# A float32 down product by seven block products in place of eight, on one Trainium2 core

## The chip, the core and the metric

The kernel runs on one core of one Trainium2 chip. It is one launch, with all inputs and outputs in HBM. The metric is the device time of the whole launch in microseconds (us); the profile adds the span, which is the time from the first to the last instruction on the core. Engines are named as in the profile: PE (TensorE), DVE (VectorE), ACT (ScalarE), POOL (GpSimd), SP (SyncE, here only a DMA queue). SBUF is the memory of the core's tiles, PSUM the accumulator memory that PE writes.

## What is computed

The reference is one step of a hybrid decoder layer over 576 tokens (512 of a prompt, 64 of requests), all in float32. Its first two thirds (input product, state space and attention branches, output product) are not touched by the change. What matters is the gated feed-forward layer at the end:

```python
h = rms_norm(x, g_ffn)
x = x + (jax.nn.silu(h @ w_gate_l) * (h @ w_up_l)) @ w_down_l
```

With `D` = 2048 model channels and `DFF` = 5632 hidden channels, the last product takes a hidden matrix g of 5632 x 576 (44 tiles of 128 channels, kept transposed) to 2048 x 576 (16 tiles of 128 channels).

## The kernel before, in words

**Precision.** A float32 product is made from three passes. Each operand is split into a rounded part and the rest: `split(hi, lo, src)` is an ACT copy (line 93) and a DVE subtraction `lo = src - hi` (line 96). For each pair of tiles PE then runs `hi*hi`, `hi*lo` and `lo*hi`. A matmul here has 128 x 128 weights and 288 tokens (`HALF`), so that one tile of 128 input channels by 128 output channels over all 576 tokens costs six matmuls.

**The gated layer** (lines 1775 to 1861) already uses Strassen's scheme in Winograd's form: tokens, input and output channels are each cut in two, and seven block products replace eight. The combined weights are made on DVE, and the results are combined on DVE out of PSUM. POOL does one multiplication `u<-u` of 128x576 for each tile of g and sends the tile to DRAM (`g_d`).

**The down product** (lines 1866 to 1912) is plain. The 44 tiles of g are taken in ranges: first 4 tiles, then five ranges of 8. In each range a loop runs over the 16 output tiles m; one job (m, range) is 4 or 8 input tiles by six matmuls into a pair of PSUM banks `pg`, and its evacuation `down_evac` is one DVE addition of 128x576 into the running sum `x1T` in SBUF, which starts as the layer's input. Weights come as `raw` tiles of four input tiles (128x512, 256 KB) from `w_down`; `advance` loads up to four and splits up to two ahead of the job that uses them. The next range's tiles of g are loaded (`g_in`, tile `u`) and split (`ghl`) between the jobs of the running range. After the last range, each finished row m is turned by five PE transposes, copied out of PSUM and stored; `pump` puts that work between the matmuls of later jobs. POOL has no work in the down product.

The order of instructions is set by a scheduling layer, which takes the program and orders each engine's instructions by priorities and buffers; each engine then runs its own list strictly in that order, and waits where a wait stands. So what follows an instruction in an engine's list also waits for it.

```python
def split(hi, lo, src):
    act(hi, src)
    tt(lo, src, hi, OP.subtract)
...
ranges = [(0, 4)] + [(k, k + 8) for k in range(4, nf, 8)]
...
x = x1T[:, m]
tt(v2(x), ps, v2(x), OP.add)
```

Of the kernel before, what the change touches and what calls it, by code (L numbers as in the profile page):

```python
# [37 lines left out]
class Pump:  # L38
    """Interleaves the emission of side work with the main stream of products."""
# [37 lines left out]
def hybrid_step_kernel(ctx, tc, x_prompt, x_sample, cache_k, cache_v, cache_win_k, cache_win_v,  # L77
# [164 lines left out]
    # rows of the paged caches to gather  # L242
# [52 lines left out]
    def rsqrt_small(x, scale):  # L295
        """(x * scale + eps) ** -0.5 in place for a few columns."""
        n = x.shape[1]
        ts(x, x, scale, OP.mult, EPS, OP.add)
        tt(x, x, mhalf[:x.shape[0], :n], OP.pow, G)

    def spread(out, r5):
        """Columns of tokens [128, 5] as rows on all partitions."""
        for s in range(2):
            ps = pt()
            for i, j in enumerate(((0, 1, 2, 3), (4,))[s]):
                n = 128 if j < 4 else TS
                tp(ps[:, i * 128:i * 128 + n], r5[:n, j:j + 1].to_broadcast([n, 128]), ident[:n, :n])
            (act if s == 0 else V.tensor_copy)(out[:, :TP] if s == 0 else out[:, TP:T], ps[:, :TP if s == 0 else TS])
# [54 lines left out]
    # =========================================================== products with the weights  # L363
# [40 lines left out]
    def run_group(group, ratio, before=None):  # L404
        """Emits the products of the group's jobs, side work of `ratio` times their time between them."""
        pss = [pt()[:, None, :] if j.small else pg() for j in group]
        n_k = sum(c[0] for c in group[0].chunks)
        k0 = 0
        for ci in range(len(group[0].chunks)):
            if before:  # L410
                before(ci)
            for job, ps in zip(group, pss):
                m = job.m
                nk, _, rhs = job.chunks[ci]
                i = state["i"]
# [12 lines left out]
        for job, ps in zip(group, pss):  # L428
            job.evac(ps[:job.m, :, :HALF])
# [26 lines left out]
    # =========================================================== keys, values, queries  # L456
# [166 lines left out]
    # =========================================================== constants used by the mixers  # L623
# [25 lines left out]
    def k_cmp_norm(pc, n):  # L649
        """RMS-normed rows (without the gain) of the compressed keys pc [n, 256]."""  # L650
# [88 lines left out]
    def tail(src, u, n, pa, hb, w2):  # L739
        """The second layer of a unit of blocks, and what becomes of its rows."""  # L740
# [39 lines left out]
    # =========================================================== attention of the new tokens  # L780
# [5 lines left out]
    def masked_bias(out, pattern, base, lim, cmp):  # L786
        """-slope * distance, far below any score where the distance fails the test."""
# [8 lines left out]
    def softmax_rows(s_, n, mx, gate, sums):  # L796
        """exp(s - max) * gate / sum in place over the first n columns of s_."""
# [9 lines left out]
    def sample_attn():  # L807
# [69 lines left out]
        # gates by row (g, r, i)  # L877
# [8 lines left out]
        # compressed branch of all requests, and the block that each row leaves out  # L886
# [33 lines left out]
        for b in range(8):  # L920
# [62 lines left out]
            def weigh(tiles, last=False):  # L983
                """tiles: (rows of P, its key count, the values)."""
# [71 lines left out]
    def to_ext(E, ps, w, rst):  # L1056
        """Columns of a product, scaled, into prompt and request rows with room for w - 1 earlier ones."""
# [59 lines left out]
    def ssd():  # L1117
# [70 lines left out]
        for c in range(5):  # L1188
# [3 lines left out]
            # token-major x * dt, its decayed copy, and B  # L1192
# [127 lines left out]
    # =========================================================== short convolution  # L1320
# [28 lines left out]
    # =========================================================== attention within the prompt  # L1349
    pp = None  # L1350

    def prompt_attn():
# [13 lines left out]
        def split_q(p, qb):  # L1366
            """For each half of the channels: the upper parts of its queries in its own partitions, the lower in the others."""
# [11 lines left out]
        for p in range(2):  # L1379
# [14 lines left out]
            for qb in range(4):  # L1394
# [4 lines left out]
                # compressed branch, eight heads at once  # L1399
# [182 lines left out]
    def slot(h, j, dt=F32):  # L1582
        """Channel tiles j and j + 8 of one half of the tokens, and then an operand's two parts in their place."""
# [55 lines left out]
    # ---- the gated layer's two products by Winograd's seven products of 2 x 2 blocks: the tokens, the output and  # L1639
    # the input channels are each cut in two; the operands of the tokens' side stay, those of the weights' side pass  # L1640
# [4 lines left out]
    def early(g):  # L1645
        """The first two products of group g, those that need the first half of the tokens only."""
# [219 lines left out]
    # ---- back to the model's channels  # L1866
# [3 lines left out]
    ranges = [(0, 4)] + [(k, k + 8) for k in range(4, nf, 8)]  # L1870
    gs = {}

    def g_in(f_):
        t_ = evt(T)
        nc.sync.dma_start(t_, g_d[f_])
        hl = fp.tile([128, 2, T], F32R, name="ghl", tag="ghl", bufs=16)
# [3 lines left out]
    def down_evac(m, last):  # L1880
        def f(ps):
            x = x1T[:, m]
            tt(v2(x), ps, v2(x), OP.add)
            if not last:
                return
            ot = evt(512).rearrange("p (a b) -> p a b", a=4)
            ots = fp.tile([TS, 128], F32, name="ots", tag="ots", bufs=2)

            def fin():
                yield  # L1890
                ps = pt()
                for j in range(4):
                    tp(ps[:, j * 128:(j + 1) * 128], x[:, j * 128:(j + 1) * 128], ident)
                act(ot, ps.rearrange("p (a b) -> p a b", a=4))
                ps = pt()
                tp(ps[:TS, :128], x[:, TP:T], ident)
                V.tensor_copy(ots, ps[:TS, :128])
                nc.sync.dma_start(dram(y_prompt, m * 128, [[D, 128], [128 * D, 4], [1, 128]]), ot)
                nc.sync.dma_start(dram(y_sample, m * 128, [[D, TS], [1, 128]]), ots)
                yield  # L1900
            pump.add(fin())
        return f

    jobs6 = [[Job(w_chunks(cols_src(w_down, D, m * 128, row0=k0 * 128), lambda k, k0=k0: gs[k0 + k], k1 - k0), 128,
                  down_evac(m, k1 == nf)) for m in range(KT)] for k0, k1 in ranges]
    for j in jobs6:
        add_jobs(j)
    for f_ in range(*ranges[0]):
        g_in(f_)
    for m in range(0, KT, 4):  # L1910
        nc.sync.dma_start(x1T[:, m:m + 4], x1_d[m:m + 4].rearrange("k p t -> p k t"))
    for n, j in enumerate(jobs6):
        nxt = list(range(*ranges[n + 1])) if n + 1 < len(ranges) else []
        for m, job in enumerate(j):
            if nxt and m >= 1 and m % (2 if n else 1) == 0:
                g_in(nxt.pop(0))
            run_group([job], 0.3)
        for f_ in nxt:
            g_in(f_)
    pump.drain()  # L1920
    close_pool(fg)
    close_pool(x1g)
    close_pool(fwg)
# [30 lines left out]
```

## Time and profile before

| | |
|---|---|
| median of 3 runs | 2958.08 us (2955.71 to 2959.1) |
| span of the profiled execution | 2957.9 us |
| PE busy | 2894.8 us, 98% of the span |
| DVE busy | 1867.6 us, 63% |
| ACT busy | 1158.4 us, 39% |
| POOL busy | 579.3 us, 20% |
| down product, first matmul to end of span | 2371.2 to 2957.9 us |

The profiled execution is one more execution than the three runs; its span, 2957.9 us, lies inside their range, and no other time is known of it. A busy share says how long an engine had an instruction in work over the whole span; since the program has stages with different limits, the stretch of the down product is read by itself.

### The profile page before, as it was taken

The numbers are of one execution on the slowest core, as the hardware profiler recorded it, in microseconds if no ns is written. First come the engines' busy times: TensorE is split into PE (matmuls) and PEld (weight loads), VectorE is DVE, ScalarE is ACT, GpSimd is POOL, SyncE is SP. The second block draws the span as 40 slices with busy tenths as digits, with TensorE's granted clock in tenths as the row PEclk, the third lists the DMA queues.
The fourth block names the chain that finished last, engine by engine and source line by source line (L and its number), as shares of the span: only waits on it lengthen the run. The fifth ranks groups of instructions, "written<-read, shape, count | busy, mean of one in ns | idle before, by whom it ended". The sixth has DMA issues, their size and how long they took to land.

```text
span 2957.9 us, 56793 instructions
## 1 busy us (share of the span) xinstructions
PE 2894.8 (98%) x22226; PEld 2749.9 (93%) x22226; DVE 1867.6 (63%) x3790; ACT 1158.4 (39%) x2140; POOL 579.3 (20%) x624
## 2 busy tenths in 40 slices
PE   7999999999999999998999999999999989999999
PEld 6998999888777898998999999999999989999999
DVE  5454444567767657568898888888788753333332
ACT  4353344334545423255444444444444431222222
POOL 3525321664333202023111011011011000000000
PEclk9999999999999999999999999999999999999999
DMA  7434344765121144375553333333333272332333
GB/s 224 128 106 137 103 106 107 223 217 125 52 62 39 41 136 138 108 226 161 175 173 115 101 109 111 107 109 109 105 112 110 73 243 84 115 116 83 95 99 95
DMA packets 467189, 360.89 MB, mean 122 GB/s; under 512 B 64458, under 2 KB 427953, under 8 KB 466921
## 3 DMA queue, kind: packets, MB, share of 16 engines
q1 hardware_dynamic: 443800, 297.89, 33.8%
q0 software_dynamic: 20336, 54.09, 6.1%
q10 hardware_dynamic: 2784, 5.29, 0.5%
q8 instruction: 175, 2.87, 0.4%
q14 instruction: 94, 0.76, 0.1%
HBM read 304.46 MB, written 50.61 MB: 120 GB/s over the span
## 4 chain that ended last, share of the span: by engine, by line
PE 57%; DVE 2%; DMA 1%; issue 0%; ACT 0%; POOL 0%; ACTq 0%; DVEq 0%; POOLq 0%
PE pg L424 24%; PE pg L1834 17%; PE pt L1834 9%; PE po L1834 5%; DVE wlo L96 1%; PE pt L424 1%; PE pt L124 1%; PE pt L120 0%; DVE x L105 0%; DVE X L96 0%; DMA u<-g_d 0%; DVE x L96 0%; DMA raw<-in_w_up_dram 0%; PE po L120 0%; DVE raw L96 0%
## 5 line engine op out<-in xcount | busy, mean ns | idle before, releaser
L93 ACT ACTIVATE whi<-raw 128x512 fp32r<-128x512 f32 x729 | 457.8, 629 | 982.5 <-PE pg L424 679.7
L96 DVE TENSOR_TENSOR wlo<-raw,whi 128x512 fp32r<-128x512 f32 x729 | 507.7, 698 | 394.3 <-ACT whi L93 369.0
L424 PE MATMUL pg<-ghl,whi 128*128 128x288 f32 x2816 | 495.7, 297 | 8.5 <-ACT ghl L93 8.1
L424 PEld LDWEIGHTS pg<-ghl,whi 128*128 128x128 f32 x2816 | 415.4, 189 | 9.4 <-ACT ghl L93 8.5
L424 PE MATMUL pg<-hhi,whi 128*128 128x288 f32 (+1 forms) x1440 | 338.2, 314 | 5.1 <-DVE u L96 3.4
L424 PE MATMUL pg<-hlo,whi 128*128 128x288 f32 (+1 forms) x1440 | 322.0, 302 | 1.1 <-DVE hlo L105 1.1
L424 PE MATMUL pg<-hhi,wlo 128*128 128x288 f32 (+1 forms) x1440 | 316.4, 300 | 0.0
L424 PE MATMUL pg<-ghl,wlo 128*128 128x288 f32 x1408 | 302.4, 296 | 0.0
L424 PEld LDWEIGHTS pg<-hhi,whi 128*128 128x128 f32 (+1 forms) x1440 | 235.6, 191 | 28.2 <-issue 14.3
L1834 PE MATMUL pt<-X,fhi 128*128 128x288 f32 x1280 | 258.5, 296 | 0.0
L1834 PE MATMUL pg<-X,fhi 128*128 128x288 f32 x1232 | 246.7, 294 | 0.0
L424 PEld LDWEIGHTS pg<-hlo,whi 128*128 128x128 f32 (+1 forms) x1440 | 234.5, 190 | 8.6 <-issue 5.3
L424 PEld LDWEIGHTS pg<-hhi,wlo 128*128 128x128 f32 (+1 forms) x1440 | 234.1, 190 | 3.3 <-issue 3.2
L96 POOL TENSOR_TENSOR u<-u 128x576 f32<-128x576 f32 x44 | 68.9, 1566 | 824.7 <-DVE u L96 794.0
L424 PEld LDWEIGHTS pg<-ghl,wlo 128*128 128x128 f32 x1408 | 226.1, 189 | 0.0
L93 ACT ACTIVATE fhi<-wr 128x512 fp32r<-128x512 f32 x225 | 142.2, 632 | 189.3 <-PE pt L1834 107.1
L96 DVE TENSOR_TENSOR flo<-wr,fhi 128x512 fp32r<-128x512 f32 x225 | 197.6, 878 | 13.7 <-ACT fhi L93 11.5
L1834 PEld LDWEIGHTS pt<-X,fhi 128*128 128x128 f32 x1280 | 205.8, 188 | 0.0
L1834 PEld LDWEIGHTS pg<-X,fhi 128*128 128x128 f32 x1232 | 197.8, 188 | 0.0
L424 PE MATMUL pg<-S,whi 128*128 128x288 f32 x1024 | 197.1, 300 | 0.0
L1834 PE MATMUL pt<-X,flo 128*128 128x288 f32 x640 | 189.2, 296 | 0.0
L96 DVE TENSOR_TENSOR x1T<-pg,x1T 128x576 f32<-128x576 f32 x96 | 72.7, 757 | 180.6 <-PE pg L424 180.6
(1308 smaller groups left out, 5768.1 us busy)
## 6 DMA issues: line engine op xcount, KB each, us to landing
wr<-in_w_gate_dram SPq DMA_DIRECT2D x88, 512.0 KB
wr<-in_w_up_dram SPq DMA_DIRECT2D x88, 512.0 KB
raw<-in_w_down_dram SPq DMA_DIRECT2D x176, 256.0 KB
raw<-in_w_in_dram SPq DMA_DIRECT2D x144, 256.0 KB
raw<-in_w_out_dram SPq DMA_DIRECT2D x64, 256.0 KB
g_d<-u POOLq DMA_DIRECT2D x44, 288.0 KB, 2.9
u<-g_d SPq DMA_DIRECT2D x44, 288.0 KB
raw<-in_w_in_dram SPq DMA_DIRECT2D x64, 128.0 KB
```

What stands on the lines that cost most here:

```text
L93: S.activation(out, in_, func, bias=bias, scale=scale, accum_out=accum)
L96: (eng or V).tensor_tensor(out, a, b, op=op)
L124: PE.transpose(out, in_, ident)
L424: PE.matmul(ps[:m, s, :HALF], w[:, k, :m], x[:, s * HALF:(s + 1) * HALF], start=(k0 + k == 0 and n == 0), stop=(k0 + k == n_k - 1 and n == 2))
L1834: PE.matmul(P[n], w[:, k, :], xx, start=(j == 0 and q_ == 0), stop=(j == 7 and q_ == 2))
```

## The change

The first four tiles of g stay plain (`jobs6`, `g_plain`, `plain_evac`). The other 40 are taken in `NR` = 5 ranges of eight, and each range in 8 items (r, mp): an item has two output tiles (m, m+1), two blocks of four input tiles and both halves of the tokens, which is a 2 x 2 block product made by seven products of 4 tiles by 3 passes, 12 matmuls each, 84 an item. Its order is `ORDER` = "1256473".

- **Weights:** `w_ops` forms four combined weight tiles of 128x512: s1, s3 and s4 on POOL, s2 on DVE. It then splits seven weight tiles (four raw, three combined ones are used beside s1: "1", "2", "4" are raw; "5", "6", "7", "3" are s1, s2, s3, s4). Each item's operands are made during the item before.
- **Tokens' side:** `g_op` forms for each of four tile pairs and each of the seven products an operand of 128x288: four POOL operations (tile `gt`) and seven splits (tile `go`) for a pair, so 16 and 28 for a range. The first range's are made beside the plain jobs, the others in the last two items of the range before.
- **Sums:** `evac_d` adds each product to the parts of `x1T` it belongs to: one ACT copy into `u`, six DVE operations that read PSUM (five of 128x288, one of 128x576) and three POOL additions into `x1T` (two of 128x288, one of 128x576).
- **Output:** `out_rows` turns and stores two rows at the end of each item of the last range, no longer by `pump`.
- The pool `fw` is closed before the pools of the down product are opened. Comments and docstrings are removed as well, which moves line numbers.

The core of the diff:

```diff
-    ranges = [(0, 4)] + [(k, k + 8) for k in range(4, nf, 8)]
+    close_pool(fwg)
...
+    NP = 4
+    NR = (nf - NP) // 8
+    GO = 32
...
+    ORDER = "1256473"
...
+    def g_op(r, j, n):
...
+        if n == "5":
+            tt(x, b12, b11, OP.subtract, G)
+        elif n == "6":
+            tt(x, b22, x, OP.subtract, G)
+        elif n == "4":
+            tt(x, b21, x, OP.subtract, G)
+        elif n == "7":
+            tt(x, b22, b12, OP.subtract, G)
+        x = {"1": b11, "2": b21, "3": b22}.get(n, x)
+        o = fp.tile([128, 2, HALF], F32R, name="go", tag="go", bufs=GO)
+        split(o[:, 0], o[:, 1], x)
...
+    def w_ops(i):
...
+        s1, s2, s3, s4 = [wpool.tile([128, KC, 128], F32, name="raw", tag="raw", bufs=4) for _ in range(4)]
+        tt(s1, a21, a22, OP.add, G)
+        tt(s3, a11, a21, OP.subtract, G)
...
+            if n == "6":
+                tt(s2, s1, a11, OP.subtract)
+                tt(s4, a12, s2, OP.subtract, G)
...
+            split(hi, lo, src)
...
+    def evac_d(i, n, p, u):
...
+        if n == "1":
+            act(u, p)
+            tt(x11, x11, u, OP.add, G)
+        elif n == "2":
+            tt(x11, p, x11, OP.add)
+        elif n == "5":
+            x2 = x1T[:, m:m + 2, HALF:]
+            tt(x2, p[:, None, :].to_broadcast([128, 2, HALF]), x2, OP.add)
+        elif n == "6":
+            tt(u, p, u, OP.add)
+            tt(x12, x12, u, OP.add, G)
+        elif n == "4":
+            tt(x21, p, x21, OP.add)
+        elif n == "7":
+            tt(u, p, u, OP.add)
+            x2 = x1T[:, m + 1].rearrange("p (h t) -> p h t", h=2)
+            tt(x2, x2, u[:, None, :].to_broadcast([128, 2, HALF]), OP.add, G)
+        else:
+            tt(x12, p, x12, OP.add)
...
+            evac_d(i, n, p, u)
+            next(nxt, None)
+            if last and q_ < 6:
+                for j in range(4):
+                    g_op(r + 1, j, ORDER[q_ + 1])
+        if r == NR - 1:
+            out_rows(2 * mp)
+            out_rows(2 * mp + 1)
```

**Where it moves instructions.** DVE in the down product before: two weight splits (`wlo`) for each evacuation into `x1T`.

```order
L96 TENSOR_TENSOR x1T_28209<-pg_29186,x1T_28209 128x576 [waits PE_49]
L96 TENSOR_TENSOR wlo_29282<-raw_29217,whi_29281 128x512 [waits DMAHW2_49,Activation_49]
L96 TENSOR_TENSOR wlo_29319<-raw_29249,whi_29318 128x512 [waits DMAHW3_49,PE_49,Activation_49]
L96 TENSOR_TENSOR x1T_28209<-pg_29248,x1T_28209 128x576 [waits PE_49]
L96 TENSOR_TENSOR wlo_29349<-raw_29279,whi_29348 128x512 [waits DMAHW4_49,Activation_49]
```

DVE now, within one item of the second product onwards (`pt`, `pg`, `po` are the PSUM tiles of the products; `wlo` and `flo` the rests of split weights; `raw_29520` is s2 of a later item).

```order
L96 TENSOR_TENSOR x1T_28210<-pt_29361,x1T_28210 128x288 [waits PE_49,Pool_49]
L96 TENSOR_TENSOR wlo_29402<-wr_29211,whi_29401 128x512 [waits DMAHW6_49,Activation_49]
L96 TENSOR_TENSOR x1T_28210<-pt_29362,x1T_28210 128x2x288 [waits PE_49]
L96 TENSOR_TENSOR wlo_29419<-raw_29378,whi_29418 128x512 [waits Activation_49]
L96 TENSOR_TENSOR u_29357<-pg_29358,u_29357 128x288 [waits DMASW1_49,PE_49]
L96 TENSOR_TENSOR flo_29439<-raw_29379,fhi_29438 128x512 [waits Activation_49]
L96 TENSOR_TENSOR x1T_28210<-pg_29358,x1T_28210 128x288 [waits PE_49]
L96 TENSOR_TENSOR flo_29456<-wr_29211,fhi_29455 128x512 [waits Activation_49]
L96 TENSOR_TENSOR u_29357<-po_29363,u_29357 128x288 [waits PE_49,Pool_49]
L96 TENSOR_TENSOR flo_29474<-raw_29380,fhi_29473 128x512 [waits Activation_49]
L96 TENSOR_TENSOR raw_29520<-raw_29519,wr_29353 128x512 [waits DMAHW7_49,DVE_49]
L96 TENSOR_TENSOR x1T_28210<-pg_29359,x1T_28210 128x288 [waits PE_49]
```

The next row is the split of s4 (`flo_29491<-raw_29381`), and after it the first split of the following item. Evacuations and splits alternate; the first row waits for POOL's addition into the same part of `x1T`.

POOL in the same item, where it had nothing before: the addition after product 1, s1 of a later item, the addition after product 6, s3, the addition after product 7, s4, and the first row of the next item.

```order
L96 TENSOR_TENSOR x1T_28210<-x1T_28210,u_29357 128x288 [waits Activation_49]
L96 TENSOR_TENSOR raw_29519<-wr_29353,wr_29355 128x512 [waits DMAHW7_49,DMAHW0_49,DVE_49]
L96 TENSOR_TENSOR x1T_28210<-x1T_28210,u_29357 128x288 [waits DVE_49]
L96 TENSOR_TENSOR raw_29521<-wr_29353 128x512 [waits DVE_49,Pool_49]
L96 TENSOR_TENSOR x1T_28210<-x1T_28210,u_29357 128x576 [waits DVE_49]
L96 TENSOR_TENSOR raw_29522<-wr_29355,raw_29520 128x512 [waits DVE_49]
L96 TENSOR_TENSOR x1T_28210<-x1T_28210,u_29498 128x288 [waits Activation_49]
```

By the values of their waits, s1 waits until DVE has split the s1 before it (`wlo_29419`), whose buffer it takes; s4 waits for the split of the s4 before it (`flo_29491`), the last DVE operation of the item; and the next item's addition stands behind s4.

POOL at the end of a range, in its last item: between the same operations now stand 12 operations on `gt` for the next range.

```order
L96 TENSOR_TENSOR x1T_28210<-x1T_28210,u_29933 128x288 [waits Activation_49]
L96 TENSOR_TENSOR gt_29993<-gr_28918,gt_29993 128x288 [waits DVE_49]
L96 TENSOR_TENSOR gt_29998<-gr_29062,gt_29998 128x288 [waits DVE_49,Activation_49]
L96 TENSOR_TENSOR gt_30003<-gr_29206,gt_30003 128x288 [waits DVE_49]
L96 TENSOR_TENSOR gt_30008<-gr_29350,gt_30008 128x288 [waits DVE_49]
L96 TENSOR_TENSOR raw_30194<-wr_29929,wr_29931 128x512 [waits DMAHW0_49,DMAHW7_49,DVE_49,Pool_49]
L96 TENSOR_TENSOR gt_29993<-gr_28918,gt_29993 128x288 [waits DVE_49]
```

Each `gt` operation overwrites the tile that DVE has just split, so it waits for DVE, and DVE's next splits wait for it by way of ACT.

## Rows read from the trace of the kernel before

**Rows 1.** Page, part 1: engine, busy us, share of the span, instructions
```profile
PE 2894.8 (98%) x22226; PEld 2749.9 (93%) x22226; DVE 1867.6 (63%) x3790; ACT 1158.4 (39%) x2140; POOL 579.3 (20%) x624
```
**Rows 2.** Page, part 4: the chain that ended last, by engine
```profile
PE 57%; DVE 2%; DMA 1%; issue 0%; ACT 0%; POOL 0%; ACTq 0%; DVEq 0%; POOLq 0%
```
**Rows 3.** Busy time by stretch: PE, PEld, DVE, ACT, POOL, PEclk, DMA share, GB/s
```profile
1380.00:1446.00 66.00, 57.07 (x385) 54.07 (x386) 58.02 (x101) 34.94 (x76) 18.84 (x20) 0.95 0.51 157
...
2000.00:2300.00 300.00, 300.00 (x2259) 300.00 (x2258) 247.33 (x389) 129.98 (x214) 29.61 (x28) 1.00 0.34 108
2371.00:2440.00 69.00, 62.59 (x449) 61.89 (x450) 38.50 (x57) 23.44 (x38) 3.02 (x4) 0.95 0.75 250
2440.00:2940.00 500.00, 500.00 (x3764) 499.73 (x3764) 178.48 (x269) 120.56 (x192) 0.00 (x0) 1.00 0.34 100
```
**Rows 4.** Groups on DVE, down product: xcount, busy us, mean ns, idle before
```profile
L96 DVE TENSOR_TENSOR wlo<-raw,whi 128x512 fp32r<-128x512 f32 x174 | 120.6, 693 | 162.5 <-ACT whi L93 162.5
L96 DVE TENSOR_TENSOR x1T<-pg,x1T 128x576 f32<-128x576 f32 x96 | 72.7, 757 | 180.6 <-PE pg L424 180.6
```
**Rows 5.** Timeline, gated layer, PE: start us, us; starts of two products
```profile
1907.76 0.43 PE L1834 MATMUL pg<-x,whi 128*128 128x288 f32 x2
...
1909.35 0.43 PE L1834 MATMUL po<-x,whi 128*128 128x288 f32 x2
```
**Rows 6.** Timeline, gated layer, POOL: two multiplications of one group
```profile
1700.85 1.42 POOL L96 TENSOR_TENSOR u<-u 128x576 f32<-128x576 f32 x1 [39.58 <-DVE u L96]
...
1703.33 1.75 POOL L96 TENSOR_TENSOR u<-u 128x576 f32<-128x576 f32 x1 [0.18 <-issue]
```
**Rows 7.** Timeline, the same stretch, DVE
```profile
1700.25 0.81 DVE L96 TENSOR_TENSOR u<-po,u 128x288 f32<-128x288 f32 x2
1701.12 1.70 DVE L96 TENSOR_TENSOR flo<-wr,fhi 128x512 fp32r<-128x512 f32 x1
1702.73 0.45 DVE L96 TENSOR_TENSOR u<-pg,u 128x288 f32<-128x288 f32 x1
1703.10 0.68 DVE L96 TENSOR_TENSOR raw<-wr,raw 128x512 f32<-128x512 f32 x1
1703.70 1.92 DVE L96 TENSOR_TENSOR flo<-wr,fhi 128x512 fp32r<-128x512 f32 x1
```
**Rows 8.** Groups on DVE in the gated layer, 1600 to 2300 us
```profile
L96 DVE TENSOR_TENSOR flo<-wr,fhi 128x512 fp32r<-128x512 f32 x189 | 166.0, 878 | 10.3 <-ACT fhi L93 8.5
```
**Rows 9.** One tile's operations on POOL: ns min/median/max, first and last start
```profile
L96 POOL TENSOR_TENSOR x<-x x8: 791/806/1191, 1371.8 to 1435.8; 128x288 f32<-128x288 f32 x8
...
L96 POOL TENSOR_TENSOR cr<-cr,xc x8: 735/1292/1802, 1126.8 to 1174.5; 128x512 f32<-128x512 f32 x6, 128x256 f32<-128x256 f32 x2
...
L96 POOL TENSOR_TENSOR sq_a<-sq_a,u x3: 1412/1424/1426, 1011.7 to 1106.5; 128x576 f32<-128x576 f32 x3
```
**Rows 10.** Timeline, DVE, two subtractions of 128x288 from SBUF
```profile
1391.76 0.45 DVE L96 TENSOR_TENSOR X<-x,X 128x288 fp32r<-128x288 f32 x1
1392.12 0.45 DVE L96 TENSOR_TENSOR raw<-x,x 128x288 f32<-128x288 f32 x1
```
**Rows 11.** Timeline, output product, POOL and then DVE: an addition that waits
```profile
1331.30 2.35 POOL L96 TENSOR_TENSOR rstdB<-rstdB,u 128x288 f32<-128x288 f32 x1 [2.77 <-ACT u L93]
...
1331.57 0.81 DVE L96 TENSOR_TENSOR X<-x,X 128x288 fp32r<-128x288 f32 x2
1332.31 0.68 DVE L96 TENSOR_TENSOR wlo<-raw,whi 128x512 fp32r<-128x512 f32 x1
1332.91 1.06 DVE L105 SCALAR_TENSOR_TENSOR x<-x,cols,rstdB 128x288 f32<-128x288 f32 x1
```
**Rows 12.** Timeline, end of the span: last sum, transposes, copy
```profile
2951.86 0.76 DVE L96 TENSOR_TENSOR x1T<-pg,x1T 128x576 f32<-128x576 f32 x1 [5.05 <-PE pg L424]
2952.67 0.77 PE L124 MATMUL pt<-ident,x1T 128*128 128x128 f32 x5 [0.85 <-DVE x1T L96]
2953.37 0.60 ACT L93 ACTIVATE u<-pt 128x512 f32<-128x512 f32 x1 [6.35 <-PE pt L124]
```

More of the change, by code (lines that the diff above doesn't have):

```diff
@@ L1869, in hybrid_step_kernel, with out_rows @@
     fg, fp = open_pool("ffn", side="right")
-    ranges = [(0, 4)] + [(k, k + 8) for k in range(4, nf, 8)]
+    NP = 4
+    NR = (nf - NP) // 8
+    GO = 32
     gs = {}
-    def g_in(f_):
+    def out_rows(m):
+        x = x1T[:, m]
+        ot = evt(512).rearrange("p (a b) -> p a b", a=4)
+        ots = evt(128)[:TS]
+        ps = pt()
+        for j in range(4):
+            tp(ps[:, j * 128:(j + 1) * 128], x[:, j * 128:(j + 1) * 128], ident)
+        act(ot, ps.rearrange("p (a b) -> p a b", a=4))
+        ps = pt()
+        tp(ps[:TS, :128], x[:, TP:T], ident)
+        act(ots, ps[:TS, :128])
+        nc.sync.dma_start(dram(y_prompt, m * 128, [[D, 128], [128 * D, 4], [1, 128]]), ot)
+        nc.sync.dma_start(dram(y_sample, m * 128, [[D, TS], [1, 128]]), ots)
@@ L1874, in g_in, with g_plain, g_load @@
+    def g_plain(f_):
         t_ = evt(T)
         nc.sync.dma_start(t_, g_d[f_])
-        hl = fp.tile([128, 2, T], F32R, name="ghl", tag="ghl", bufs=16)
+        hl = fp.tile([128, 2, T], F32R, name="ghl", tag="ghl", bufs=4)
         split(hl[:, 0], hl[:, 1], t_)
         gs[f_] = hl[:, 0], hl[:, 1]
-    def down_evac(m, last):
+    ORDER = "1256473"
+    raws, ops = {}, {}
+    def g_load(r, j):
+        t_ = fp.tile([128, 2, T], F32, name="gr", tag="ghl", bufs=4)
+        for h in range(2):
+            nc.sync.dma_start(t_[:, h], g_d[NP + 8 * r + 4 * h + j])
+        raws[r, j] = t_[:, 0], t_[:, 1]
@@ new lines, in evac_d @@
+    def evac_d(i, n, p, u):
+        m = items[i][1] * 2
+        x11, x21, x12 = x1T[:, m, :HALF], x1T[:, m + 1, :HALF], x1T[:, m, HALF:]
+        if n == "1":
[17 more added lines that the diff above has]
+            tt(x12, p, x12, OP.add)
@@ L1881, in f, with plain_evac @@
+    def plain_evac(m):
         def f(ps):
@@ L1883, in f @@
             tt(v2(x), ps, v2(x), OP.add)
[L1884 to L1900, printed above, removed]
@@ L1901, in f @@
-            pump.add(fin())
-        return f
[L1904 to L1909, printed above, removed]
+        return f
+    jobs6 = [Job(w_chunks(cols_src(w_down, D, m * 128), lambda k: gs[k], NP), 128, plain_evac(m)) for m in range(KT)]
+    add_jobs(jobs6)
@@ L1910, in hybrid_step_kernel, with first_ops @@
+    for f_ in range(NP):
+        g_plain(f_)
     for m in range(0, KT, 4):
         nc.sync.dma_start(x1T[:, m:m + 4], x1_d[m:m + 4].rearrange("k p t -> p k t"))
[L1912 to L1920, printed above, removed]
+    def first_ops():
+        for j in range(4):
+            raws[0, j] = evt(T), evt(T)
+            for h in range(2):
+                nc.sync.dma_start(raws[0, j][h], g_d[NP + 4 * h + j])
+            for n in ORDER:
+                g_op(0, j, n)
+                yield
@@ new lines, in hybrid_step_kernel @@
+    side = first_ops()
+    for m, job in enumerate(jobs6):
+        run_group([job], 0.0)
+        for _ in range(2):
+            next(side, None)
+        if m == 9:
+            load_d(0)
+            load_d(1)
+    for _ in side:
+        pass
+    for _ in w_ops(0):
+        pass
+    for i, (r, mp) in enumerate(items):
+        last = mp == KT // 2 - 1 and r + 1 < NR
+        if mp < 4 and r + 1 < NR:
+            g_load(r + 1, mp)
+        if mp == KT // 2 - 2 and r + 1 < NR:
+            for j in range(4):
+                g_op(r + 1, j, ORDER[0])
+        load_d(i + 2)
+        nxt = w_ops(i + 1) if i + 1 < len(items) else iter(())
+        u = evt(HALF)
+        pa, pb = pg(), pg()
+        ps = [pt()[:, :HALF] for _ in range(3)] + [pa[:, 0, :HALF], pa[:, 1, :HALF], po()[:, :HALF], pb[:, 0, :HALF]]
+        for q_, n in enumerate(ORDER):
+            p = ps[q_]
+            hi, lo = made[i].pop(n)
+            for j in range(KC):
+                o = ops[r, j, n]
+                for c_, (w, x) in enumerate(((hi, o[:, 0]), (hi, o[:, 1]), (lo, o[:, 0]))):
+                    PE.matmul(p, w[:, j, :], x, start=(j == 0 and c_ == 0), stop=(j == 3 and c_ == 2))
+            evac_d(i, n, p, u)
+            next(nxt, None)
+            if last and q_ < 6:
+                for j in range(4):
+                    g_op(r + 1, j, ORDER[q_ + 1])
+        if r == NR - 1:
+            out_rows(2 * mp)
+            out_rows(2 * mp + 1)
@@ L1921, in hybrid_step_kernel @@
     close_pool(fg)
     close_pool(x1g)
-    close_pool(fwg)
     close_pool(eg)
```

28 lines of the change are left out of this document (added).

## The prediction

> **What bounds the kernel now.** I read the busy shares first, then the chain of waits, then the stretch of the down product by itself. PE is busy for 98% of the span [rows 1], and the chain that ended last names PE far ahead of every other engine [rows 2]. In the down product PE is busy for all 500 us between 2440 and 2940 at a granted clock of 1.00, with DVE busy for 178 us, ACT for 121 and POOL for nothing [rows 3]. DVE's own groups there say the same from the other side: before the splits it was idle waiting for ACT, before the additions into `x1T` for PE, 181 us in sum [rows 4]. So one matmul less is worth its full time, as long as the others keep up.
>
> **What is saved.** One product of 12 matmuls follows the one before it by 1.59 us [rows 5], 132.5 ns a matmul. Before, 44 input tiles by 16 output tiles by 6 are 4224 matmuls. Now the four plain tiles take 384 and the 40 items 84 each, 3360, in sum 3744. That is 480 fewer, 480 x 0.1325 = **63.6 us saved** on PE. An item's PE time is 7 x 1.59 = 11.15 us.
>
> **What an item asks of DVE and POOL.** From start to start DVE needs 0.60 us for a 128x512 operation from SBUF and 0.37 for 128x288 out of PSUM [rows 7], so some 0.67 for 128x576 out of PSUM, whose mean is 757 ns [rows 4] less the 0.08 by which such rows overlap. An item has eight of the first (seven splits and s2), five of the second, one of the third: 4.8 + 1.85 + 0.67 = 7.3 us. POOL's medians are 1.29, 0.81 and 1.42 us for 128x512, 128x288 and 128x576 [rows 9]; three, two and one of them make 6.9 us. Seven ACT copies and one from PSUM are below 5 us at the 0.60 us of [rows 12]. Each sum is below 11.15, so by busy time alone PE would stay the bound. The trace says that they may not be added side by side.
>
> **DVE and POOL exclude each other.** In [rows 6, 7] POOL's multiplication runs from 1700.85 to 2.27. DVE's split, which needs 0.69 us otherwise, starts at 1701.12 and ends at 2.82, 0.55 after POOL. The second time POOL starts at 1703.33 inside DVE's `raw` operation and takes 1.75 us in place of 1.42, ending 1.30 after DVE's end; the next split waits for it and takes 1.92. Over the gated layer this lifts the mean of such splits to 878 ns [rows 8] from 693 [rows 4]. The additions out of PSUM are not touched (0.81 for two beside POOL [rows 6, 7]). So a DVE operation with both inputs in SBUF and a POOL operation with two inputs run one after the other: a POOL operation right behind DVE costs 0.12 less than its own time, a DVE split right behind POOL 0.55.
>
> The Trainium skill says this as a rule against the change, in "SBUF — State Buffer", section "Who interferes with whom": a DVE instruction with two SBUF inputs contends with a GpSimd instruction that reads SBUF, and whoever issues first holds the shared pair for the whole instruction. By that rule turns alternate wherever both wait. The trace agrees in [rows 6, 7], but not everywhere: in [rows 11] the POOL addition that starts at 1331.30 needs 2.35 us in place of 0.81, while three further DVE operations pass it. By the rule my item below is 12.6 us long; by that row POOL can lose a turn where two DVE operations follow each other, which is at two places of an item and adds 0.6, 13.2 us. I take 12.6, since evacuations stand between the other splits.
>
> **One item laid out.** The two lists in the section on the change, from the end of the addition after product 1, in us: DVE evacuates 2, splits, evacuates 5, splits: 0.1 + 0.37 + 0.60 + 0.67 + 0.60 = 2.3, and POOL stands, because s1 takes the buffer of the last split. Then s1 1.29, at 3.6, 3.8 with both handovers (evacuation 6 beside it); split 0.55, 4.3; addition after 6, 0.68, 5.0 (evacuation 4 beside it); split 0.55, 5.5; s3 1.17, 6.7 (evacuation 7); split 0.55, 7.2; addition after 7, 1.30, 8.5; s2 0.55, 9.1; evacuation and the last split 0.97, 10.0. Only now may s4 start: it waits for that split, and DVE's next one takes the turn first, 0.6. s4 1.17, 11.8; the next item's first addition 0.80, **12.6 us**. It stands behind s4, and DVE's next evacuation waits for it, so this circle closes. The operands are made an item ahead, but that lead is used once and not again. PE waits 12.6 - 11.15 = 1.45 us an item. For the 32 items of the first four ranges that is **+46 us**. Bounds: 11.6 if half of POOL's waiting falls beside other work (+14), 13.2 as above (+66).
>
> **Ends of ranges.** Four times the next range's operands are made inside two items: 28 splits of 128x288 from SBUF, 0.37 each from start to start [rows 10], 10.4 us on DVE, and 16 POOL operations of 0.68 behind DVE, 10.9 us. These exclude each other and the rest. Some 3 us fit where POOL or DVE stood in the layout above, so 18 us each, **+72 us**. Bounds: 12, DVE's splits and a little, if POOL's work fits in gaps; 23, if none fits. The first range's operands are made beside the plain jobs, 51 us of PE time in which DVE has 16 x (0.60 + 0.67) = 20 us of its own: nothing, as DVE's 10 and POOL's 13 us more still leave room; without that cover 21 us.
>
> **Last range.** `out_rows` stands at the end of its own item, where PE waits for the last additions, turns (0.77 us for five transposes) and waits for ACT's copy (0.60) before it may use the PSUM tiles again [rows 12]. Half of a product stands ahead of the transposes. From the end of the last product: additions 2.0, transposes and copy 1.5, less 0.5: an item is 11.15 + 3.0, some 14.2 us. The transposes, 1.1 an item, were there before, so 2 us each, 16 us for eight: **+16**. Bounds 8 and 32 (additions done at once; POOL's s3 and addition both still ahead). The start of the stage is alike: PE stood 6.4 of 69 us before [rows 3], waiting for g, and waits for the same tiles now. Loads stay at 256 KB for 4 tiles by 128 columns; at 100 GB/s they cover the stage now [rows 3] and in fewer, larger pieces then. Both count as nothing, and two or three us either way.
>
> **Sum.** Against the profiled span: 2957.9 - 63.6 + 46 + 72 + 16 = 3028.3, **3028 us**. The span lies 0.2 below the median of the runs, which changes nothing. About 0.2%, 6 us, is what a measurement can tell from no change.
>
> **The rivals.**
> *Side by side.* If DVE and POOL overlap in these shapes, each is under 7.5 us an item and PE stays the bound: 2957.9 - 63.6 + 16 + 11 (a little at the range ends) = 2921. For it: evacuations out of PSUM are free of POOL, and the operands are an item ahead. Against it: every split of [rows 7] beside POOL is longer by 1.0 to 1.2 us. Chance 0.14.
> *Only the ends of ranges.* If the items keep pace with PE at 11.15 because the circle through s4 is shorter than I lay it out, PE still has the lead of about 9.5 us at each range end, 18 - 9.5 = 8.5 remains, four times: 2957.9 - 63.6 + 34 + 16 = 2944. It decides from 1.45 us of hidden waiting an item. Chance 0.11.
> *The clock falls.* PE stands for 12% of each item and for more at the ends. In [rows 3] the two stretches where PE was idle for 9 and 14% of the time show a granted clock of 0.95, the full ones 1.00. At 0.95 an item needs 11.7 on PE, still under 12.6, and costs nothing. At 1.2 GHz all through it would need 22.3; with 10 of 40 items so, 10 x 9.7 = 97 more, 3125. Chance 0.05. The Trainium skill, "TensorE: Matmul & The Clock Gate", section "HAM oscillation — how this bites in real kernels", tells of a kernel whose clock falls again and again as PE waits for each tile. No stretch here shows that.
> That the change would not make seven products is no rival: the built order has 84 matmuls an item.
>
> **How the numbers follow.** The forecast has 0.70: 0.05 of it within 6 us of no change, at its low ends together (14 + 48 + 8 against 63.6: 2964), the rest slower, up to 66 + 92 + 32 - 63.6 = 126 above, 3084. Faster are the first two rivals, 0.25. Slower: 0.65 + 0.05 = 0.70. The range goes from halfway between the two rivals, 2932, since the second one's range ends may cost less than 8.5, to just below the high end, 3080; outside lie side by side and the fallen clock, 0.19.
>
> **What would show it.** In the changed profile: 3744 matmuls in the stage; splits of 128x512 with a mean well above 0.9 us in place of 0.69; POOL over 300 us busy there; the wait of PE named by DVE or ACT and not by DMA; an item every 12.6 us inside a range and about 30 at its end. Wrong I would be if splits stay at 0.7 beside POOL, or if an item takes 11.2 us with PE full.

## The result, and the profile after

The changed kernel takes **3044.74 us** (median of four runs, 3043.27 to 3050.36) against 2957.11 before in the same comparison: a ratio of 1.0295, 95% interval 1.028 to 1.031. Slower was forecast, 3028 us; the time lies in the range, 17 us above the forecast. The span of the profiled execution is 3043.1 us, 85.2 more than before; nothing ahead of the down product explains it, since the product starts 5.1 us earlier than before. I call the time from its first matmul to the end of the span **the stage**: 586.7 us before (2371.2 to 2957.9), 676.9 now (2366.2 to 3043.1).

The page's first part and its chain by engine, after:

```profile
PE 2876.5 (95%) x21746; PEld 2715.7 (89%) x21746; DVE 2191.5 (72%) x4194; ACT 1269.6 (42%) x2416; POOL 983.6 (32%) x944
...
PE 43%; DVE 9%; POOL 4%; issue 3%; DMA 1%; ACT 1%; SPq 0%; POOLq 0%; ACTq 0%; DVEq 0%
```

Against [rows 1] PE has its 480 matmuls less, but only 18 us less busy time, mostly since part of the matmuls runs at a lower clock (the end of a range, below); DVE has 324 us more and POOL 404. In the chain DVE and POOL have taken part of PE's place [rows 2].

Busy time by stretch, after: PE, PEld, DVE, ACT, POOL, PEclk, DMA share, GB/s. The first stretch is four items inside a range, the second from product 1 of the range's last item to that of the next item, the third the three items that follow:

```profile
2477.06:2529.22 52.16, 45.92 (x338) 44.99 (x337) 41.96 (x57) 19.87 (x36) 31.99 (x24) 1.00 0.25 83
2529.22:2554.19 24.97, 17.48 (x114) 17.24 (x113) 24.97 (x35) 11.76 (x30) 19.60 (x18) 0.79 0.15 46
2554.19:2597.80 43.61, 35.37 (x227) 34.24 (x226) 40.33 (x51) 15.79 (x30) 30.88 (x23) 0.88 0.37 123
```

Where [rows 3] has PE at 500 of 500 us, it now has 45.9 of 52.2: 52.16 / 4 = **13.04 us an item**, of which PE needs 11.15. The end of the range, 24.97 + 43.61 = 68.58 us for four items, is 68.58 - 52.16 = **16.4 us** longer than four others. In the first of these two stretches DVE is busy from end to end.

The items' operations on POOL and then DVE, in one item (start us, us), and behind them one row of PE and one of ACT; each record of POOL and DVE includes the time that the operation was held:

```profile
2478.44 1.68 POOL L96 TENSOR_TENSOR raw<-wr,raw 128x512 f32<-128x512 f32 x1 [1.60 <-DVE flo L96]
2480.08 0.81 POOL L96 TENSOR_TENSOR x1T<-x1T,u 128x288 f32<-128x288 f32 x1
2483.32 1.27 POOL L96 TENSOR_TENSOR raw<-wr 128x512 f32<-128x512 f32 x1 [2.43 <-DVE wlo L96]
2484.55 1.25 POOL L96 TENSOR_TENSOR x1T<-x1T,u 128x288 f32<-128x288 f32 x1
2485.77 1.29 POOL L96 TENSOR_TENSOR raw<-wr 128x512 f32<-128x512 f32 x1
2488.05 1.81 POOL L96 TENSOR_TENSOR x1T<-x1T,u 128x576 f32<-128x576 f32 x1 [1.00 <-DVE u L96]
```
```profile
2478.28 0.68 DVE L96 TENSOR_TENSOR wlo<-wr,whi 128x512 fp32r<-128x512 f32 x1
2480.92 0.46 DVE L96 TENSOR_TENSOR x1T<-pt,x1T 128x288 f32<-128x288 f32 x1 [1.96 <-POOL x1T L96]
2481.30 0.68 DVE L96 TENSOR_TENSOR wlo<-wr,whi 128x512 fp32r<-128x512 f32 x1
2481.89 0.75 DVE L96 TENSOR_TENSOR x1T<-pt,x1T 128x576 f32<-128x576 f32 x1
2482.56 0.68 DVE L96 TENSOR_TENSOR wlo<-raw,whi 128x512 fp32r<-128x512 f32 x1
2483.16 0.45 DVE L96 TENSOR_TENSOR u<-pg,u 128x288 f32<-128x288 f32 x1
2483.53 1.61 DVE L96 TENSOR_TENSOR flo<-raw,fhi 128x512 fp32r<-128x512 f32 x1
2485.58 0.46 DVE L96 TENSOR_TENSOR x1T<-pg,x1T 128x288 f32<-128x288 f32 x1 [0.44 <-PE pg L2040]
2486.17 1.44 DVE L96 TENSOR_TENSOR flo<-wr,fhi 128x512 fp32r<-128x512 f32 x1
2487.53 0.45 DVE L96 TENSOR_TENSOR u<-po,u 128x288 f32<-128x288 f32 x1
2487.90 0.68 DVE L96 TENSOR_TENSOR flo<-raw,fhi 128x512 fp32r<-128x512 f32 x1
2488.61 1.81 DVE L96 TENSOR_TENSOR raw<-raw,wr 128x512 f32<-128x512 f32 x1
```
```profile
2483.66 0.53 PE L2040 MATMUL pg<-go,fhi 128*128 128x288 f32 x2 [1.57 <-DVE u L96]
...
2485.50 0.63 ACT L93 ACTIVATE fhi<-wr 128x512 fp32r<-128x512 f32 x1 [3.48 <-PE pg L2040]
```

A split beside no POOL operation takes 0.68; the one of 2483.53, in POOL's s1, ends 0.55 behind it, as in [rows 6, 7]; the addition of 2484.55 is held by that split and takes 1.25 in place of 0.81. Evacuations of 128x288 out of PSUM take 0.45 or 0.46 everywhere in the item. And DVE stands 1.96 us before 2480.92, since POOL's addition comes behind the s4 that started at 2478.44: the circle that closes an item.

PE stands once in an item, for 1.57 us right before product 4 (2483.66): it is released by DVE's evacuation of product 6 (`u<-pg,u`, 2483.16), which reads the other half of the same tile `pg`. So product 4 ends late, DVE waits 0.44 for it, and ACT's copy for split 4 (`fhi<-wr`) starts at 2485.50.

The same in DVE's and POOL's groups over the stage, 2370 to 3043 us (xcount, busy us, mean ns, idle before): a split of a combined tile takes 1044 ns where [rows 4] had 693.

```profile
L96 DVE TENSOR_TENSOR flo<-raw,fhi 128x512 fp32r<-128x512 f32 x120 | 124.9, 1044 | 1.1 <-ACT fhi L93 0.7
...
L96 POOL TENSOR_TENSOR x1T<-x1T,u 128x576 f32<-128x576 f32 x40 | 72.0, 1801 | 40.6 <-DVE u L96 39.6 <-DVE x1T L96 1.0
```

The end of a range on PE (start us, us, idle before it): two matmuls of a row took 0.42 before the stand, 0.68 for 5 us after it. That is the lower of the clock's two levels, 1.2 GHz, after 7.49 us without work; the first of the two stretches behind these rows, in the columns used above, has a granted clock of 0.50. The second, 0.51, follows a stand of only 1.83 us in the plain tiles.

```profile
2535.75 0.42 PE L2040 MATMUL pg<-go,fhi 128*128 128x288 f32 x2
...
2543.93 0.85 PE L2040 MATMUL pg<-go,fhi 128*128 128x288 f32 x2 [7.49 <-DVE u L96]
2544.57 0.44 PE L2040 MATMUL pg<-go,flo 128*128 128x288 f32 x1
2544.81 0.68 PE L2040 MATMUL pg<-go,fhi 128*128 128x288 f32 x2
```
```profile
2429.81 1.22 PE L424 MATMUL pg<-ghl,whi 128*128 128x288 f32 x4 [1.83 <-DVE x1T L96]
```
```profile
2543.93:2549.00 5.07, 5.07 (x21) 5.07 (x22) 5.07 (x5) 1.09 (x3) 5.07 (x6) 0.50 0.00 0
2429.80:2433.00 3.20, 3.19 (x14) 3.20 (x15) 2.74 (x4) 0.00 (x0) 0.32 (x1) 0.51 0.35 118
```

### The profile page after: what moved, and what is told of

The parts are those of the page before. It is cut to its first block, busy times and chain, and to the rows that moved or that the text cites. A ratio compares the mean times of both kernels' runs of the same rounds, so it can differ in the third digit from the quotient of the medians.

```text
span 3043.1 us, 56976 instructions
## 1 busy us (share of the span) xinstructions
PE 2876.5 (95%) x21746; PEld 2715.7 (89%) x21746; DVE 2191.5 (72%) x4194; ACT 1269.6 (42%) x2416; POOL 983.6 (32%) x944
## 4 chain that ended last, share of the span: by engine, by line
PE 43%; DVE 9%; POOL 4%; issue 3%; DMA 1%; ACT 1%; SPq 0%; POOLq 0%; ACTq 0%; DVEq 0%
PE pg L1834 17%; PE pt L1834 9%; PE pg L424 5%; PE po L1834 5%; DVE go L96 3%; PE pg L2040 2%; DVE wlo L96 2%; POOL x1T L96 2%; PE pt L2040 2%; POOL raw L96 2%; DVE flo L96 1%; DVE x1T L96 1%; PE pt L424 1%; DVE u L96 1%; ACT fhi L93 1%
## 5 line engine op out<-in xcount | busy, mean ns | idle before, releaser
L93 ACT ACTIVATE whi<-raw 128x512 fp32r<-128x512 f32 (+1 forms) x609 | 381.8, 629 | 630.7 <-PE pg L424 292.2
L96 DVE TENSOR_TENSOR wlo<-raw,whi 128x512 fp32r<-128x512 f32 (+1 forms) x609 | 426.6, 702 | 231.0 <-ACT whi L93 203.8
L2040 PE MATMUL pg<-go,fhi 128*128 128x288 f32 x960 | 217.4, 318 | 90.1 <-DVE u L96 82.7
L93 ACT ACTIVATE fhi<-wr 128x512 fp32r<-128x512 f32 x265 | 167.3, 631 | 296.5 <-PE pt L1834 107.2
L96 DVE TENSOR_TENSOR flo<-wr,fhi 128x512 fp32r<-128x512 f32 x265 | 247.3, 933 | 17.4 <-ACT fhi L93 12.0
L2040 PEld LDWEIGHTS pg<-go,fhi 128*128 128x128 f32 x960 | 165.9, 203 | 99.4 <-DVE u L96 90.8
L96 DVE TENSOR_TENSOR flo<-raw,fhi 128x512 fp32r<-128x512 f32 x227 | 199.4, 881 | 51.0 <-ACT fhi L93 50.3
L93 ACT ACTIVATE fhi<-raw 128x512 fp32r<-128x512 f32 x227 | 142.6, 630 | 180.5 <-PE pg L1834 68.9
L2040 PE MATMUL pt<-go,whi 128*128 128x288 f32 x960 | 202.6, 305 | 0.0
```

The lines of the kernel that those rows point to most:

```text
L93: S.activation(out, in_, func, bias=bias, scale=scale, accum_out=accum)
L96: (eng or V).tensor_tensor(out, a, b, op=op)
L2040: PE.matmul(p, w[:, j, :], x, start=(j == 0 and c_ == 0), stop=(j == 3 and c_ == 2))
```

## The experiments

The theory: DVE operations with two SBUF inputs and POOL operations take turns, the turns and the circle through s4 fill the item, and PE waits. The rivals: DVE has too much to do whatever POOL does; or the waits for buffers are the cause and not the turns. The first four runs fell on a chip on which the kernel before took 3068.42 us, and their down product began 109 to 114 us later than in the profile above; so runs are compared by their stage, and by time only with the kernel before on the same chip. For these four the two measures differ by 0.1 to 4.5 us. Each run is one execution, but for the one with all edits.

**Weight sums on DVE.**

```diff
-        tt(s1, a21, a22, OP.add, G)
-        tt(s3, a11, a21, OP.subtract, G)
+        tt(s1, a21, a22, OP.add)
+        tt(s3, a11, a21, OP.subtract)
...
-                tt(s4, a12, s2, OP.subtract, G)
+                tt(s4, a12, s2, OP.subtract)
```

> The three weight sums s1, s3 and s4 move from POOL to DVE; POOL keeps the three additions into x1T. Theory (DVE and POOL take turns, and the circle through s4 sets the item): POOL's share of the turns falls from 6.9 to 3.0 us and the circle is gone; DVE has 11 x 0.60 + 2.5 = 9.1 us, so an item comes back to PE's 11.2 to 11.5 us, splits beside no POOL operation take 0.68, and the time is about 2990 us. Rival (DVE has simply too much to do, and PE waits for it): three more operations of 0.60 on DVE make the item 14.8 us, about 3100 us.

Stage 622.7 us, 54 less than the changed kernel; 3103.57 us beside 3068.42. Four items inside a range, the same columns:

```profile
2586.24:2633.68 47.44, 45.94 (x339) 45.02 (x338) 45.87 (x69) 19.48 (x37) 15.19 (x12) 1.00 0.29 90
```

47.44 / 4 = 11.86 us an item: three operations more on DVE, and the item is 1.2 us shorter. That DVE simply has too much falls. It is 0.4 above my expectation of 11.2 to 11.5; DVE is busy or held for 45.87 of the 47.44 us, as POOL's three additions still take turns.

**More buffers.** Two of the four combined tiles get a ring of their own:

```diff
-        s1, s2, s3, s4 = [wpool.tile([128, KC, 128], F32, name="raw", tag="raw", bufs=4) for _ in range(4)]
+        s1, s3 = [wpool.tile([128, KC, 128], F32, name="raw", tag="raw", bufs=4) for _ in range(2)]
+        s2, s4 = [fp.tile([128, KC, 128], F32, name="cw", tag="cw", bufs=4) for _ in range(2)]
...
-    GO = 32
+    GO = 28
```

> The four combined weight tiles get eight buffers in place of four (paid for with four fewer operand tiles of g, so that the first operands of a range are made after product 1 of the last item, which touches the range ends alone). Rival (only the waits for buffers, s1 and s4 for the split before them, make the item long): 11.2 to 11.5 us an item inside a range, about 2995 us. Theory (the turns of DVE and POOL fill the item): 4.8 us of DVE and 6.9 of POOL remain one behind the other, 11.7 and the handovers; an item of 12.0 to 12.8 us, about 3020 to 3045 us.

Stage 691.7 us; four items inside a range:

```profile
2844.50:2898.61 54.11, 45.92 (x339) 45.00 (x338) 39.86 (x58) 19.91 (x36) 34.54 (x24) 1.00 0.25 79
```

13.53 us an item: the buffers gain nothing, and the rival of the buffers falls. It is above the range I gave (12.0 to 12.8). One row of PE and one of DVE from an item show a wait that the layout didn't have:

```profile
2851.59 0.53 PE L2038 MATMUL pg<-go,fhi 128*128 128x288 f32 x2 [2.05 <-DVE u L96]
```
```profile
2853.48 0.46 DVE L96 TENSOR_TENSOR x1T<-pg,x1T 128x288 f32<-128x288 f32 x1 [1.35 <-PE pg L2038]
```

PE stands 2.05 us for the evacuation of product 6 before it may begin product 4 in the other half of the tile, and DVE then 1.35 us for product 4. Here the item's chain runs through PE as well. No run takes away this wait alone.

**Sums in PSUM.** PE adds products 6 and 7 onto product 1, in the same bank:

```diff
-            p = ps[q_]
+            p = ps[0 if n in "67" else q_]
...
-                    PE.matmul(p, w[:, j, :], x, start=(j == 0 and c_ == 0), stop=(j == 3 and c_ == 2))
+                    PE.matmul(p, w[:, j, :], x, start=(n not in "67" and j == 0 and c_ == 0), stop=(j == 3 and c_ == 2), skip_group_check=True)
...
-            act(u, p)
-            tt(x11, x11, u, OP.add, G)
+            tt(x11, p, x11, OP.add)
```

Products 6 and 7 are added the same way, p straight into `x12` and into row m+1. First with POOL's weight sums, then with the weight sums on DVE as well:

> Products 6 and 7 are accumulated by PE on top of product 1 in its PSUM bank, so that each sum goes from PSUM into x1T by DVE alone; ACT's copy, two DVE operations on u and the three POOL additions fall away; POOL keeps the three weight sums. Theory: the turns are 4.8 + 3.9 = 8.7 us and the handovers, the evacuations (3.2 us) need no turn; an item of 11.2 to 11.6 us, about 2985 us. Rival (the three weight sums on POOL and their waits make the item, not the additions): about 13 us an item as now, about 3040 us.

> Both edits of the other two runs: sums accumulated in PSUM, and the weight sums on DVE. POOL has nothing inside a range. Theory: DVE has 11 x 0.60 + 3.2 = 9.8 us an item, nothing to take turns with, PE is full at 11.15 us an item; range ends still add some 16 us each, the last range 2 us an item: 2957.9 - 63.6 + 64 + 16 = about 2975 us. Rival (DVE has too much to do): an item of 13 us or more, over 3030 us.

Stages 603.3 and 568.9 us; times 3080.51 and 3050.70 beside 3068.42. A stretch inside a range of the first and of the second, then a range end of the second:

```profile
2566.00:2621.00 55.00, 55.00 (x416) 55.00 (x415) 54.55 (x75) 22.02 (x35) 19.35 (x15) 1.00 0.31 97
```
```profile
2569.00:2624.00 55.00, 55.00 (x416) 55.00 (x415) 51.78 (x90) 22.12 (x35) 0.00 (x0) 1.00 0.31 96
2624.00:2677.00 53.00, 48.10 (x343) 47.05 (x342) 52.39 (x94) 26.34 (x57) 18.05 (x16) 0.97 0.36 116
```

Both have PE full inside a range, as the theory said; the edit also takes product 6 out of the tile of product 4, so the wait of PE between the two is gone along with POOL's additions. The second is 17.7 us below the kernel before in one run, where I had expected 17 above: its stage of 569 us would have been some 604 by my sum, in which each range end was put at 16 us. From the start of the sixth item of one range to that of the next, PE's 672 matmuls take 97.0, 98.5 and 98.7 us, and eight items of 11.17 would be 89.4: such an end costs 8 to 9 us.

**One term at a time, from the changed kernel.** The output rows later, and the sums of g on DVE:

```diff
+            if r == NR - 1 and mp and q_ in (3, 5):
+                out_rows(2 * mp - 2 + (q_ == 5))
...
-        if r == NR - 1:
-            out_rows(2 * mp)
-            out_rows(2 * mp + 1)
+    out_rows(KT - 2)
+    out_rows(KT - 1)
```

> Only the place of the output rows changes: in the last range the two rows of an item are turned behind products 4 (row m) and 7 (row m+1) of the next item, no longer at the end of their own. Theory (PE stands at the end of each item of the last range for POOL's and DVE's last sums, then for its transposes' copies): the items of the last range, 15.4 to 17.0 us now, come down to the 13.0 of the other ranges, some 16 us less in all; the stage of the down product, 676.9 us from its first matmul to the end of the span, becomes about 660. Rival (DVE and POOL set these items too, and the transposes only fill PE's idle time): no change, 674 to 680.

Stage 661.9 us: 15.0 less, where 16 was expected. Where the rows stand costs what the theory said.

```diff
-            tt(x, b12, b11, OP.subtract, G)
+            tt(x, b12, b11, OP.subtract)
```

(and the same for the other three sums)

> Only the 16 sums of g for each next range move from POOL to DVE (all else as in the changed kernel). Theory (POOL's 16 operations take turns with DVE's splits at a range end): 10.9 us and more on POOL become 5.9 on DVE, a range end falls from some 16.5 to 10 to 12 us, the stage of 676.9 us to about 655. Rival (DVE's splits alone make the range end, POOL's sums fit in gaps): 5.9 us more on DVE for each of four ends, about 700.

Stage 667.9 us, 9.0 less: neither. One tile's rows on PE, of the changed kernel and of this run, show where the 9 us come from; the plain tiles' matmuls take from the first to the last start:

```profile
L424 PE MATMUL pg<-ghl,whi x256: 290/295/609, 2366.2 to 2434.2; 128*128 128x288 f32 x128
```
```profile
L424 PE MATMUL pg<-ghl,whi x256: 292/295/606, 2369.6 to 2429.4; 128*128 128x288 f32 x128
```

68.0 us against 59.8: the plain tiles, beside which the first range's operands are made, and where I had put them down as nothing, are 8.2 us shorter. The first three items take 2.5 us of this back, and the rest of the 9.0 is 0.5 to 1.1 at each end. So the range ends hardly changed: what POOL's sixteen operations took in turns, sixteen more on DVE take as well.

**The remaining terms together**, from the run with the sums in PSUM and on DVE: the sums of g earlier, then the output rows later too.

```diff
+            if q_ == 2 and 2 <= mp < 6 and r + 1 < NR:
+                g_sums(r + 1, mp - 2)
```

(`g_sums` is the four subtractions on DVE, into tiles of their own.)

> From the run with the sums in PSUM and the weight sums on DVE, whose stage took 568.9 us: the sums of g for the next range are made on DVE in the third to sixth item of the running range, not in its last two. Theory (turns of POOL and DVE and the chain over gt make the range ends, 7.8 us each there): DVE has 10.9 us an item in four items, still under PE's 11.15, and a range end falls to 3 to 5 us; the stage to some 555. Rival (the 28 splits alone make the ends): 566 to 572.

> All edits together: sums accumulated in PSUM, weight sums on DVE, sums of g early on DVE, output rows behind products 4 and 7 of the next item. By the theory PE is the bound again: plain tiles 64, 40 items of 11.15, 8 x 1.1 of transposes, range ends 4 x 4, a tail of 6: a stage of 541 to 550 us against 586.7 before, so about 1.4% faster than the kernel before. Rival (something else of the scheme, such as loads or the clock, keeps the gain away): no faster than the run without the last two edits, 0.6%.

Stages 561.2 and 556.3 us. The first gains 7.7, half of what I expected, and not evenly: from the sixth item of one range to that of the next the times are 91.3, 97.5 and 98.2 us, so that 5.8 us lie at the first range end and 0.5 to 1.0 at each of the two after it. The sums of g are not what makes those later ends; the 28 splits remain there, but they stand at the first end too, which now costs 1.9 us, so the cause stays open. The second, all edits, takes **2928.66 us** (2925.01 to 2929.36) against 2956.68 before: a ratio of 0.9908, 95% interval 0.989 to 0.9925. It beats both kernels, though by less than the 1.4% I had expected. Inside a range, a range end, and the last range:

```profile
2446.00:2502.00 56.00, 56.00 (x416) 55.31 (x416) 54.94 (x104) 20.88 (x34) 0.00 (x0) 1.00 0.29 94
2600.00:2650.00 50.00, 46.24 (x325) 43.68 (x326) 49.07 (x98) 26.21 (x57) 0.00 (x0) 1.00 0.41 132
2845.00:2905.00 60.00, 60.00 (x457) 59.44 (x456) 51.43 (x89) 27.93 (x55) 0.00 (x0) 1.00 0.36 106
```

PE is full but for the range ends, where DVE is (49.07 of 50).

**The turns by themselves.** From the kernel with sums in PSUM and on DVE, whose POOL is idle inside a range, three kernels give POOL work whose result nobody reads:

```diff
+            if q_ < 6:
+                act(junk[:, 0, :1], p[:, :1])
+                tt(junk, idb, idb, OP.add, G)
```

In the second, two `G.memset(junk, ...)` stand in place of the addition, in the third `G.tensor_copy(junk, idb)`.

> From the run with the sums in PSUM and the weight sums on DVE (item 11.17 us, stage 568.9 us): behind each of the first six products of an item POOL adds a constant tile to itself into a scratch tile of 128x512 that nobody reads (an ACT copy of one column out of PSUM ahead of it ties it to its product). DVE's order and waits stay as they are. Theory (a POOL operation with two inputs and a DVE operation with two SBUF inputs take turns): 11 x 0.60 + 6 x 1.29 = 14.3 us of turns an item plus handovers, 14.3 to 15.5 us; a stage of about 700 us. Rival (only waits for results and buffers make DVE late, not POOL's running): an item of 11.2 us, a stage of 569 to 575.

> The same, with two memsets of the scratch tile in place of the addition, so that POOL works as often and writes as much, but reads nothing. Theory (turns are taken over reading from SBUF): splits stay at 0.69 us, an item at 11.2 us, a stage of 569 to 578. Rival (any POOL work on SBUF hinders DVE, writes too): more than 12.5 us an item, a stage over 620.

> The same, with a copy on POOL (one input) in place of the addition. Open between two readings: if every POOL operation that reads SBUF takes a turn, as the Trainium skill has it (SBUF — State Buffer, Who interferes with whom), the item grows by POOL's own time less what falls beside the evacuations, to some 13 us or more, a stage over 640 us; if only operations with two inputs do, 11.2 us and a stage of 569 to 578.

Stages 686.1, 584.6 and 604.1 us beside 568.9. For each kernel POOL's group and a group of DVE (xcount, busy us, mean ns, idle before), 2440 to 2920 us:

```profile
L96 POOL TENSOR_TENSOR u<-ident 128x512 f32<-128x512 f32 x188 | 240.2, 1286 | 169.9 <-ACT u L93 167.4
...
L96 DVE TENSOR_TENSOR raw<-wr 128x512 f32<-128x512 f32 x62 | 65.4, 1077 | 0.4
```
```profile
L2042 POOL MEMSET u<- 128x512 f32 x225 | 118.3, 527 | 159.9 <-ACT u L93 159.4
...
L96 DVE TENSOR_TENSOR raw<-wr 128x512 f32<-128x512 f32 x76 | 50.3, 683 | 0.6
```
```profile
L2042 POOL COPY u<-ident 128x512 f32<-128x512 f32 x216 | 168.8, 784 | 232.9 <-ACT u L93 232.9
...
L96 DVE TENSOR_TENSOR raw<-wr 128x512 f32<-128x512 f32 x73 | 60.8, 853 | 0.5
```

Additions that nobody needs make DVE's operation 1.08 us long in place of 0.68, and the stage 117 us longer, 117.2 / 40 = 2.9 an item (I had put it at 3 to 4). The tile that holds products 4 and 6 in the changed kernel plays no part here. Memsets of the same tile leave it at 0.683, and PE is full inside a range (the same columns as in the windows above):

```profile
2457.00:2513.00 56.00, 56.00 (x423) 56.00 (x422) 52.62 (x91) 27.30 (x65) 31.66 (x61) 1.00 0.30 95
```

The stage is 16 us longer all the same, outside my range; that lies outside the steady stretch, 4 us in the first items and 2 to 4 at each range end. The likeliest cause, the sums of g that stand behind memsets in POOL's list, is not shown.

Copies with one input do take turns: DVE's mean is 0.853 us, and a DVE operation that meets a copy ends 0.54 behind it, as a split behind an addition does:

```profile
2463.74 0.75 POOL L2042 COPY u<-ident 128x512 f32<-128x512 f32 x1 [0.78 <-ACT u L93]
```
```profile
2464.05 0.98 DVE L96 TENSOR_TENSOR raw<-wr 128x512 f32<-128x512 f32 x1
```

The stage is 35 us longer, which fits neither of the two readings I had put down (over 640 us, or 569 to 578). The first had too high a price: a copy takes 0.78 us, so the turns of an item are 11 x 0.60 + 6 x 0.78 = 11.3 us, hardly over PE's 11.17, and part of the 35 us is what memsets cost too.

Memsets that cost nothing and copies that take turns are the reading of the Trainium skill, "SBUF — State Buffer", section "Who interferes with whom", that POOL's reading counts and its writing doesn't; by the memsets (0.683) and the copies (0.853) the trace agrees.

## Why the prediction was right, and what was mis-sized

The direction and the mechanism hold. The extra over PE's own time, in the forecast's terms:

| term | forecast | measured |
|---|---|---|
| matmuls saved | -63.6 | -63.6 (3744 in the stage) |
| 32 items | 46, 1.45 each | 32 x (13.04 - 11.15) = 60 |
| four range ends | 72, 18 each | 16.4 each, 66, of which some 8 fall into the last range |
| last range | 16 | some 20 |
| start of the stage | 0 | some 3: 8.2 in the plain tiles, less 5.1 |
| sum | 70 | 85 |

- **The item** is the term that was mis-sized, by 0.44 us, 14 us over 32 items. In the layout PE held nobody up: evacuation 4 lay beside POOL's addition after product 6, DVE's split 4 came between that addition and s3, and evacuation 7 lay beside s3. In the trace PE starts product 4 only behind the evacuation of product 6, so evacuation 4 starts at 2485.58 and ACT's copy for split 4 ends at 2486.13. DVE is not ready for its turn when the addition ends at 2485.80; s3, next in POOL's list, takes it; split 4 runs behind s3, and evacuation 7, at 2487.53, comes behind that split and lies on the path. The rest follows as laid out, that much later, up to the circle through s4. That product 4 in a tile of its own would give the 0.44 back is an estimate from this layout, and no run tries it.
- **Turns.** The step that DVE and POOL exclude each other, taken from [rows 6, 7], is shown by the unneeded additions and memsets: waits alone don't do it, nor does DVE's own load.
- **Range ends** were right in size (16.4 for 18), though not for the whole of the reason: the sums of g cost about the same on DVE as on POOL, and with POOL idle inside the range an end is 8 to 9.
- **Last range.** The transposes at the end of their own item cost 15 us, shown by moving them; the rest is the circle of 13.04 us, 8 x 1.89 = 15, less the 9 us of transposes that PE's idle time hides (an estimate from the layout).
- **Start.** The first range's operands are not free: from the first plain matmul to the one behind the 384th it takes 68.4 us, but 60.2 both in the kernel before and with the sums of g on DVE, so POOL's sums cost the 8.2 there. The stage began 5.1 us earlier, which hid most of it in the sum.
- **The rivals.** Side by side fell with the first item. The ends alone fell too: no waiting hides in the item. The clock fell as a part of the range ends, 3 to 6 us at 1.2 GHz behind each stand of 5 us or more, and not in the items, whose granted clock is 1.00 with PE idle for 12% of them; what it costs at a range end was not separated. At that level matmuls start 0.24 us apart (2544.57, 2544.81), so a whole item there would have taken 84 x 0.24 = 20 us by these rows, and not the 22.3 of the prediction.

## What to carry to other kernels

Before work is given to an idle POOL, ask whether DVE has operations with two SBUF inputs in the same stretch: then, as here, the two engines' times are added, and work that fits each engine by itself may not fit. A sum of products can be left in PSUM and be added by PE, which costs DVE no turn, and here removed three POOL additions, two DVE operations and a copy per item. When work moves from the bound engine to others, count a whole item of the new one with its circle of waits, the bound engine's own waits among them, and count by itself what happens at the ends of loops: here they took as much as the items.

## What was unexpected of the hardware

- A POOL copy with one input takes turns with DVE like an addition (DVE 0.853 us in place of 0.683), while memsets of the same shape cost DVE nothing (0.683).
- After 7.49 us without a matmul PE ran 5 us at 1.2 GHz, but gaps of some 1.5 us in every item left the granted clock at 1.00. A stand of 1.83 us in the plain tiles was followed by 3.2 us at 0.51, while stands of 2.05 us in every item of the run with more buffers left it at 1.00. So the length of one stand doesn't tell by itself whether the clock falls.
